# A four-layer transformer on one core: the two parts of x at another address, modulo 256, in the feed-forward sublayers

## The chip, the core and the metric

The kernel runs on one core of a Trainium2 chip. What counts is the time of one execution on the device, in microseconds (us), as a median over runs. The engines are named as in the profile: PE is TensorE's matmul, PEld its load of the stationary operand (the weights of the array), DVE is VectorE, ACT ScalarE, POOL GpSimd, SP SyncE, which issues most of the DMAs.

## The reference

256 tokens of width 1024 go through two blocks of four layers each, in fp32. In the first block a layer is: feed-forward, mixer, feed-forward, each with a norm before and behind. In the second it is a mixer and a feed-forward.

```
for i in range(4):                                   # first block
    x = x + 0.5 * rms_norm(swiglu_ffn(rms_norm(x, g[0]), w_gate_up[i, 0], w_down[i, 0]), g[1])
    x = x + rms_norm(mixer[i](rms_norm(x, g[2]), memory), g[3])
    x = x + 0.5 * rms_norm(swiglu_ffn(rms_norm(x, g[4]), w_gate_up[i, 1], w_down[i, 1]), g[5])
...
for i in range(4):                                   # second block
    x = x + mixer_2[i](rms_norm(x))
    x = x + relu2_mlp(rms_norm(x), w_up[i], w_down[i])
```

The gated feed-forward has 2816 hidden columns, that of the second block 4096. All weights together are some 530 MB and each is used once.

## The kernel before

The residual stream x is kept transposed: 8 row blocks of 128 channels on the partitions, 256 tokens along the row. For precision every operand of a large product is split into two parts of type float32r, hi and lo, and a product is made of three: hi by hi, hi by lo, lo by hi. One product here is one instruction with a stationary operand of 128 by 128 and a moving operand of 128 by (mostly) 256. It is preceded by a weight load for it, which runs beside the product before.

```
def mm3(self, out, xs, ws, first, last):
    nc.tensor.matmul(out, xs[0], ws[0], start=first, stop=False)
    nc.tensor.matmul(out, xs[0], ws[1], start=False, stop=False)
    nc.tensor.matmul(out, xs[1], ws[0], start=False, stop=last)
```

The weights come by DMA into `raw` (3 buffers of 1 MB), ACT makes `whi` of them and DVE `wlo` (4 buffers each, in pieces of 512 columns). The parts of x are the tiles `xThi` and `xTlo`, one of each for the whole kernel. They are written at the end of a sublayer: `handoff` is called as the blocks of the output become ready, and its tasks add to x and write the parts of the next sublayer (`split_x` on ACT, `rest_x` on DVE).

A feed-forward sublayer goes in chunks of 256 hidden columns. `wide` makes the hidden columns: for 2 halves of 128 columns and 8 row blocks, the three products, with the weights stationary and x moving:

```
for j in range(nb):
    b = slice(j * P, (j + 1) * P)
    for k in range(KB):
        self.mm3(ps[:, j * S:(j + 1) * S], (wh[:, k, b], wl[:, k, b]), [z[:, k] for z in self.xTs],
                 k == 0, k == KB - 1)
```

That is 48 products a unit of weights; a gated chunk has two units (gate and up, 96 products), one of the second block has one. The hidden values are split into `hThi`, `hTlo`, and `down` multiplies the chunk before by its rows of the down matrix: 48 products, again with weights stationary and 256 tokens of h moving. The last two chunks go down together (the last down: 24 products of the first of them, then 72 with both). The first part of a sublayer (`early`, 96 products in each) runs while x still arrives. In the mixers x is stationary and the weights move, in widths of 512, 384, 280, 268 or 256 columns; their output goes through `oThi`, `oTlo` as moving operands, as h does in a feed-forward sublayer.

There are 12 feed-forward sublayers. They have 11,520 products with x moving (8 by 11 by 96 and 4 by 16 by 48) and 6528 with h moving at width 256 (the last sublayer takes h as the stationary operand instead). The mixer of the third layer of the second block (a convolution) uses `xThi`, `xTlo` as its own output tiles: 192 more.

Where the tiles lie on a partition is fixed when the program is built. By that table, modulo 256 bytes: `whi`, `wlo`, `xThi`, `xTlo` begin at 96; `hThi`, `hTlo` at 32; the two parts of the memory (`memT`) at 32; `oThi`, `oTlo` at 96 in the second and third mixer of the first block and at 32 in all others. All steps between blocks inside these tiles are multiples of 256 bytes. So the distance of the moving operand from the weights, modulo 256, is 0 for x, 192 for h, and 0 or 192 for o. Where the memory is stationary and weights move, it is 64.

Nearly all instructions are recorded through one helper, so their line in the profile is 160 whatever they do.

Of the kernel before, what the change touches and what calls it, by code (L numbers as in the profile page):

```python
# [9 lines left out]
F32R = mybir.dt.float32r  # L10
# [7 lines left out]
P = 128  # L18
D = 1024
# [29 lines left out]

HALVES = slice(0, 512), slice(512, 1024)  # L50
# [4 lines left out]
def consts():  # L55
    """masks, identity-like matrices and position tables, from the shapes alone"""
# [32 lines left out]
class Clock:  # L89
    """rough times of the engines in us, by which the order of the instructions is chosen"""  # L90
# [10 lines left out]
    def wait(self, until):  # L101
        """the chain of the current stage waits, for data from DRAM or for another chain"""
        if self.chain is not None:
            self.chain = max(self.chain, until)

    def free(self, engine, cost):
        """when the engine has time for an operation"""
        for a, b in self.idle[engine]:
            if max(a, self.now()) + cost <= b:
                return max(a, self.now())  # L110
        return max(self.busy[engine], self.now())

    def reserve(self, engine, start, cost):
        """end of an operation that can start then: it fills a gap between others where one is long enough"""
# [50 lines left out]
class Core:  # L165
    """the engines, with a clock that follows them"""
# [8 lines left out]
class Task:  # L175
    """a chain of stages that is emitted between the large products; a stage ends in a yield: of the engine that has to
    be idle for the next one, of 0 when that waits for other tasks, or of nothing"""
# [5 lines left out]
    def at(self):  # L183
        """when the next stage can begin"""
        return max(self.time, self.clock.busy[self.state] - 0.5) if self.state else self.time
# [12 lines left out]
class Net:  # L198
    def __init__(self, ctx, tc, a):
# [19 lines left out]
        self.xTs = [self.xp.tile([P, KB, S], F32R, name="xT" + n) for n in ("hi", "lo")]  # L219
        self.xT = [[z[:, :, t * P:(t + 1) * P] for z in self.xTs] for t in range(2)]  # L220
# [12 lines left out]

    def begin(self, gain):
        """loads x and the constants and prepares x for the first sublayer"""
# [52 lines left out]
    # ---- tasks  # L288
# [9 lines left out]
    def tick(self):  # L298
        """emits every stage whose inputs should be there by now, then some of the weights to come"""
# [38 lines left out]
    # ---- weights  # L338
    def cols(self, w, ranges, gain=None):
        """all 8 row blocks of the given columns of w, in two units"""  # L340
# [8 lines left out]
    def start(self, units):  # L349
        """units: what is loaded, in the order in which it is taken"""  # L350
# [17 lines left out]
    def load(self):  # L368
        """splits the weights into two exact float32r parts, a piece at a time"""
# [29 lines left out]
    def queue(self, *ins):  # L399
        """issues these behind the last of those that x waits for, on the same engine"""  # L400
        for i, last in zip(ins, self.last):
            self.behind(i, last)

    def behind(self, ins, first):
        """issues ins after first, on the same engine"""
# [4 lines left out]
    def ahead(self, n):  # L410
        """splits the next n units now, before what comes of x with the end of a sublayer"""
# [3 lines left out]
    def take(self, n, more=False):  # L415
        """the next n units; those taken before are through, unless these are more"""
# [8 lines left out]
    def mm3(self, out, xs, ws, first, last):  # L425
        """out (+)= xs.T @ ws for one row block, both as (hi, lo)"""
# [9 lines left out]
    def proj(self, t, units):  # L436
        """tile t's rows of x times the columns in units"""
# [6 lines left out]
    def out_block(self, y, d, blocks, first, last):  # L444
        """block d of y (+)= the transposed output: pairs of weights [128, 1024] and tokens [128, 256], both as (hi, lo).
        Two blocks of a bank are one group: its first product clears the bank for both."""
# [12 lines left out]
    def temp(self):  # L459
        """a row of 1024 for a short time"""  # L460
        return self.nrm.tile([P, KB, S], F32, name="yg", bufs=1).rearrange("p k n -> p (k n)")[:, :D]

    def new_y(self, alone):
        """the blocks of y, and those that share a bank as pairs; the last two have a bank each where they are needed one
        by one"""
# [4 lines left out]
    # ---- transposes  # L470
# [3 lines left out]
    def turn(self, out, src):  # L474
        """out = src transposed: moved, not rounded"""
# [7 lines left out]
    def split_T(self, src, n, pool, tag, hi=None, lo=None, gain=None):  # L483
        """src [128, n*128] in SBUF -> transposed blocks [128, n, 128] as (hi, lo), times the columns gain"""
# [20 lines left out]
    # ---- norms  # L505
    def bcast_row(self, pool, row, name, **kw):
        """a row of DRAM on every partition"""
# [4 lines left out]
    def rsqrt(self, ms, eps, out=None):  # L512
        """(ms + eps) ** -0.5; ms one AP or two to be added"""
# [11 lines left out]
    def square(self, x, scale, out):  # L525
        """out = sum of (scale * x) ** 2 along the row"""
        junk = self.nrm.tile([P, D], BF16, name="junk", bufs=1)
        self.nc.scalar.activation(junk[:, :x.shape[-1]], x, AF.Square, scale=scale, accum_out=out)

    # ---- the residual stream: x transposed, [128, 8 blocks, 256 tokens]  # L530
# [6 lines left out]
    def split_x(self, ks, g):  # L537
        """blocks of x times the gain, their first parts"""
# [5 lines left out]
    def rest_x(self, ks, g):  # L544
        """their second parts, and the squares of pairs"""
# [10 lines left out]
    def leave(self, b):  # L556
        """blocks 2 * b and 2 * b + 1 of the last x, as rows of tokens"""
# [9 lines left out]
    def arriving(self):  # L567
        """(block, part of the weights, part of x) of the products with an x that is still on its way"""
# [13 lines left out]
    def col_sums(self, pc, srcs, first, last):  # L582
        """pc [128, 2] (+)= the sums over the partitions of each [128, 256] of srcs, for each token of both tiles"""
# [6 lines left out]
    def to_rows(self, cols, warm=(0, 0), behind=None):  # L590
        """cols [128, 2], one of a token -> the same on all partitions, [128, 256] in PSUM; before and behind, products
        that nobody reads keep the clock of the tensor engine up while it waits"""
# [15 lines left out]
    def rms(self, deps):  # L608
        """mean square + eps and reciprocal rms of x"""
# [9 lines left out]
    def handoff(self, y, done, end, weight=1.0, rest=None):  # L619
        """x += weight * rms_norm(y) * gain, or x += y, then what the next sublayer needs of x; a product left the next  # L620
        block of y. end: gains of this and of the next norm; rest: mean square + eps of the x by whose rms y still has to
        be divided, or rows by which it still has to be multiplied"""
# [3 lines left out]
        if d == 0:  # L626
            self.out = {"acc": self.nrm.tile([P, 2, S], F32, name="acc", bufs=1), "after": []}
# [39 lines left out]
    def gain_y(self, y, ds, g, o):  # L667
        """blocks ds of y times the gain, and their squares"""
# [66 lines left out]
    # ---- feed-forward  # L735
    FF = 256

    def ffn_steps(self, dff, gated):
        """('part', chunks) and ('down', chunks) in their order; the first part is of two units, the last two chunks go
        down together"""  # L740
# [19 lines left out]
    def ffn(self, w_in, w_down, dff, gated, g_out, g_next):  # L760
# [4 lines left out]
        with tc.tile_pool(name="ff", bufs=3) as fp, tc.tile_pool(name="ff1", bufs=1) as f1:  # L765
# [5 lines left out]
            def scales():  # L771
                """what the reciprocal rms of x still has to be applied with: rows for the gate or for y, the rest of the
                norm of y"""
# [29 lines left out]
            def early():  # L803
                """two units side by side, for x is still on its way"""
# [11 lines left out]
            def wide():  # L816
                """columns of tokens"""
# [78 lines left out]
    # ---- attention pieces  # L896
    def scores(self, ps, q, k, mask=None, extra=()):
        """ps = q.T @ k (+ extra) (+ mask), mask is (column offset, bf16 tile)"""
# [9 lines left out]
    def exp_rows(self, pool, s, scale, den):  # L908
        """exp(scale * (s - max of s)) for each of the b rows of s [128, b, n] in PSUM, den [128, b] gets the sums;
        scale is a number or a column"""  # L910
# [16 lines left out]
    def turn_p(self, pool, p, n, tag="pT"):  # L927
        """the n transposed blocks of p [128, ...]"""
# [10 lines left out]
    def pv(self, out, pT, vs):  # L939
        """out = sum over blocks of p @ v"""  # L940
# [3 lines left out]
    def normalise(self, pool, o, den, heads, t, kb, swapped=False):  # L944
        """o [128, heads * d] in PSUM over den [128, heads], transposed, is from block kb on the input of the output
        projection"""
# [1074 lines left out]
```

## Time and profile before

| | |
|---|---|
| time, median of 3 runs | 3330.47 us (3327.56 to 3331.14) |
| span of the profiled execution, first to last instruction | 3322.9 us |
| PE busy | 3222.2 us, 97% |
| PEld busy | 3073.1 us, 92% |
| DVE busy | 2127.4 us, 64% |
| ACT busy | 1660.6 us, 50% |
| HBM read over the span | 543.82 MB, 165 GB/s |
| mean granted clock of TensorE | 0.990 |

The profiled execution's own time on the device is not listed apart from the three runs; its span is 7.6 us below their median. Matmuls are pipelined, and the ends of their records are modelled: a record of a 256-wide product is some 280 ns long while the next one starts after about 115. So PE's busy share says little. What counts is the distance from one start to the next, here called the pitch: the length of a stretch without pauses over the number of products that start in it. A window of the profile also counts the two products that started before it and are still in flight; they are subtracted.

### The profile page before, as it was taken

How to read it: one execution, taken by the hardware profiler on the slowest of the kernel's cores; microseconds unless marked ns; L12 is line 12 of the kernel's file. 1: busy time of each engine (PE TensorE's matmuls, PEld its weight loads, DVE VectorE, ACT ScalarE, POOL GpSimd, SP SyncE). 2: the span in 40 equal slices, each digit the busy share in tenths (PEclk: the TensorE clock that was granted, in tenths of full speed). 3: DMA queues.
4: the chain of work that ended last, by engine and by line, in shares of the span. 5: the costliest groups of instructions: out<-in, count | busy, mean ns of one | idle time of the engine just before them, and what ended most of it. 6: DMA issues, size and time to landing. Idle time of an engine off the chain costs nothing. (4 is left out here: it accounts for less than half of the span.)

```text
span 3322.9 us, 60453 instructions
## 1 busy us (share of the span) xinstructions
PE 3222.2 (97%) x25108; PEld 3073.1 (92%) x25108; DVE 2127.4 (64%) x3857; ACT 1660.6 (50%) x3375; POOL 261.7 (8%) x237
## 2 busy tenths in 40 slices
PE   8999999999999999999999999999999978999999
PEld 8998999998999997999998998699989967998998
DVE  6557757567757556655657756775666587657754
ACT  6445545445445445544545544554565453545643
POOL 1001000001000000000001001200100051002100
PEclk9999999999999999999999999999999998999999
DMA  7654555544455543454554554535545540554463
GB/s 267 203 183 156 169 184 172 184 127 146 161 183 171 185 153 121 140 190 165 191 190 138 195 184 127 171 123 191 182 147 183 188 142 29 188 191 147 141 197 127
DMA packets 387970, 550.88 MB, mean 166 GB/s; under 512 B 12108, under 2 KB 310956, under 8 KB 387694
## 3 DMA queue, kind: packets, MB, share of 16 engines
q1 hardware_dynamic: 372648, 534.89, 48.9%
q10 hardware_dynamic: 14694, 10.92, 1.1%
q8 instruction: 197, 3.23, 0.4%
q0 software_dynamic: 352, 1.19, 0.2%
q14 instruction: 79, 0.65, 0.1%
HBM read 543.82 MB, written 3.15 MB: 165 GB/s over the span
## 5 line engine op out<-in xcount | busy, mean ns | idle before, releaser
L160 ACT CAST whi<-raw 128x512 fp32r<-128x512 f32 x1996 | 1119.2, 617 | 1108.7 <-issue 945.7
L160 DVE TENSOR_TENSOR wlo<-raw,whi 128x512 fp32r<-128x512 f32 x1996 | 1311.2, 703 | 539.0 <-ACT whi L160 538.2
L160 PE MATMUL ps<-xThi,whi 128*128 128x256 f32 x3904 | 1060.8, 284 | 3.1 <-ACT xThi L160 2.2
L160 PE MATMUL ps<-xTlo,whi 128*128 128x256 f32 x3904 | 1057.7, 283 | 4.0 <-DVE xTlo L160 4.0
L160 PE MATMUL ps<-xThi,wlo 128*128 128x256 f32 x3904 | 1057.6, 283 | 0.0
L160 PEld LDWEIGHTS ps<-xThi,whi 128*128 128x128 f32 x3904 | 727.1, 192 | 7.3 <-ACT xThi L160 6.8
L160 PEld LDWEIGHTS ps<-xTlo,whi 128*128 128x128 f32 x3904 | 727.3, 192 | 5.9 <-DVE xTlo L160 5.4
L160 PEld LDWEIGHTS ps<-xThi,wlo 128*128 128x128 f32 x3904 | 727.4, 192 | 0.0
L160 PE MATMUL ps<-hThi,whi 128*128 128x256 f32 x2176 | 602.4, 277 | 0.0
L160 PE MATMUL ps<-hTlo,whi 128*128 128x256 f32 x2176 | 601.9, 277 | 0.0
L160 PE MATMUL ps<-hThi,wlo 128*128 128x256 f32 x2176 | 601.4, 276 | 0.0
L160 PEld LDWEIGHTS ps<-hTlo,whi 128*128 128x128 f32 x2176 | 409.2, 188 | 0.0
L160 PEld LDWEIGHTS ps<-hThi,whi 128*128 128x128 f32 x2176 | 409.0, 188 | 0.0
L160 PEld LDWEIGHTS ps<-hThi,wlo 128*128 128x128 f32 x2176 | 408.8, 188 | 0.0
L160 PE MATMUL ps<-whi,xThi 128*128 128x512 f32 (+4 forms) x688 | 255.3, 386 | 4.6 <-ACT xThi L160 4.6
L160 PE MATMUL ps<-whi,xTlo 128*128 128x512 f32 (+4 forms) x688 | 245.5, 372 | 5.0 <-DVE xTlo L160 5.0
L160 PE MATMUL ps<-wlo,xThi 128*128 128x512 f32 (+4 forms) x688 | 245.0, 372 | 2.1 <-DVE wlo L160 1.9
L160 DVE TENSOR_TENSOR act<-ps,rows 128x512 f32<-128x512 f32 x88 | 60.8, 690 | 198.9 <-PE ps L160 198.9
L160 DVE TENSOR_TENSOR h<-ps,act 128x512 f32<-128x512 f32 x88 | 60.8, 691 | 174.5 <-PE ps L160 171.3
L160 POOL TENSOR_TENSOR acc<-acc,sq 128x512 f32<-128x512 f32 x60 | 98.1, 1634 | 862.7 <-issue 645.7
L160 PEld LDWEIGHTS ps<-whi,xTlo 128*128 128x128 f32 x688 | 130.3, 191 | 26.7 <-DVE xTlo L160 7.1
L160 PEld LDWEIGHTS ps<-whi,xThi 128*128 128x128 f32 x688 | 130.4, 192 | 26.3 <-ACT xThi L160 8.2
(334 smaller groups left out, 3496.9 us busy)
## 6 DMA issues: line engine op xcount, KB each, us to landing
raw<-in_ffn_w_gate_up_dram SPq DMA_DIRECT2D x176, 1024.0 KB, 5.1
raw<-in_ffn_w_down_dram SPq DMA_DIRECT2D x88, 1024.0 KB, 4.9
raw<-in_mlp_w_up_dram SPq DMA_DIRECT2D x64, 1024.0 KB, 5.5
raw<-in_mlp_w_down_dram SPq DMA_DIRECT2D x64, 1024.0 KB, 4.9
raw<-in_a_w_in_dram SPq DMA_DIRECT2D x12, 1024.0 KB, 5.2
raw<-in_sb_w_in_dram SPq DMA_DIRECT2D x12, 1024.0 KB, 5.2
raw<-in_moba_w_in_dram SPq DMA_DIRECT2D x12, 1024.0 KB, 5.1
raw<-in_b_w_in_dram SPq DMA_DIRECT2D x36, 256.0 KB, 3.5
```

What stands on the lines that cost most here:

```text
L160: return f(*args, **kw)
```

## The change

`xThi` and `xTlo` become tiles with 64 spare elements (256 bytes) behind them, and a view of x is laid into them at an offset that `place` chooses for each sublayer, when its x begins to be written. In feed-forward sublayers it is 28 or 48 elements of 4 bytes, 112 or 192 bytes; in the mixers it is 0, and in the convolution 64 elements, 256 bytes. For `ffn` the first of a layer's two has 28 and the second 48; for `mlp` layers 0 and 2 have 28, layers 1 and 3 have 48. That makes 5760 products with x moving at distance 112 and 5760 at 192. To make room a scratch tile (`junk`) shrinks to 128 columns, and the memory's preparation has one of its own.

```
+SPARE = 64
+X_AT = {"ffn": (28, 48), "mlp": (28, 48), "mix": (0, 0), "mix2": (0, 64)}
...
-        self.xTs = [self.xp.tile([P, KB, S], F32R, name="xT" + n) for n in ("hi", "lo")]
-        self.xT = [[z[:, :, t * P:(t + 1) * P] for z in self.xTs] for t in range(2)]
+        self.room = [self.xp.tile([P, KB * S + SPARE], F32R, name="xT" + n) for n in ("hi", "lo")]
...
+    def place(self, step):
+        at = X_AT[step[0]][step[-1] % 2 if step[0] != "mix2" else step[1] == 2]
+        self.xTs = [z[:, at:at + KB * S].rearrange("p (k n) -> p k n", k=KB) for z in self.room]
+        self.xT = [[z[:, :, t * P:(t + 1) * P] for z in self.xTs] for t in range(2)]
...
     def handoff(self, y, done, end, weight=1.0, rest=None):
...
         if d == 0:
+            if self.following is not None:
+                self.place(self.following)
...
-    def square(self, x, scale, out):
-        junk = self.nrm.tile([P, D], BF16, name="junk", bufs=1)
+    def square(self, x, scale, out, junk=None):
+        if junk is None:
+            junk = self.nrm.tile([P, P], BF16, name="junk", bufs=1)
...
-                self.square(m, 1.0 / 32.0, ms)
+                self.square(m, 1.0 / 32.0, ms, mt.tile([P, D], BF16, name="junk"))
...
     net.start(units)
+    net.place(plan[0])
...
+        net.following = plan[n + 1] if n + 1 < len(plan) else None
```

The rest of the diff takes out comments. In the built programs the instructions of every engine stand in the same order, and on PE, DVE and SP each has the same waits with the same counts; ACT has one wait less and POOL two that name other DMA queues, at the preparation of the memory and of one mixer. Every tile behind `xTlo` in memory moves by a multiple of 256 bytes (1280 for those of the sublayers). So h keeps its distance of 192 and o and the memory keep theirs.

## Rows read from the trace of the kernel before

**Rows 1.** The page, part 1: busy time of PE over the span.

```profile
span 3322.9 us, 60453 instructions
...
PE 3222.2 (97%) x25108; PEld 3073.1 (92%) x25108; DVE 2127.4 (64%) x3857; ACT 1660.6 (50%) x3375; POOL 261.7 (8%) x237
```

**Rows 2.** The page, part 5: groups of products and weight loads.

```profile
## 5 line engine op out<-in xcount | busy, mean ns | idle before, releaser
...
L160 PE MATMUL ps<-xThi,wlo 128*128 128x256 f32 x3904 | 1057.6, 283 | 0.0
...
L160 PEld LDWEIGHTS ps<-xThi,wlo 128*128 128x128 f32 x3904 | 727.4, 192 | 0.0
...
L160 PE MATMUL ps<-hThi,wlo 128*128 128x256 f32 x2176 | 601.4, 276 | 0.0
...
L160 PEld LDWEIGHTS ps<-hThi,wlo 128*128 128x128 f32 x2176 | 408.8, 188 | 0.0
```

**Rows 3.** Windows of the trace: steady chunks of the first feed-forward sublayer.

```profile
core 0: us, PE busy (x) PEld busy (x) DVE busy (x) ACT busy (x) POOL busy (x), PEclk, DMA share, GB/s
91.80:239.00 147.20, 147.20 (x1251) 147.20 (x1249) 80.74 (x129) 65.66 (x121) 0.00 (x0) 1.00 0.57 187
```

**Rows 4.** Windows: one chunk's products with x, then those with h.

```profile
91.80:103.30 11.50, 11.50 (x98) 11.50 (x97) 5.68 (x9) 4.89 (x9) 0.00 (x0) 1.00 0.58 197
103.31:108.75 5.44, 5.44 (x50) 5.44 (x49) 3.70 (x6) 2.71 (x5) 0.00 (x0) 1.00 0.53 163
```

**Rows 5.** Windows: most of the last down of two feed-forward sublayers.

```profile
242.09:250.09 8.00, 8.00 (x70) 8.00 (x69) 4.89 (x11) 2.18 (x4) 0.00 (x0) 1.00 0.43 133
525.13:532.83 7.70, 7.70 (x70) 7.70 (x69) 4.79 (x11) 2.19 (x4) 0.00 (x0) 1.00 0.42 138
```

**Rows 6.** Windows of 6 us in the eleven last downs, three shown.

```profile
243.00:249.00 6.00, 6.00 (x53) 6.00 (x52) 3.10 (x7) 1.79 (x3) 0.00 (x0) 1.00 0.57 178
526.00:532.00 6.00, 6.00 (x55) 6.00 (x55) 3.26 (x7) 2.01 (x4) 0.00 (x0) 1.00 0.54 178
...
3008.80:3014.80 6.00, 6.00 (x56) 6.00 (x55) 5.05 (x9) 2.87 (x6) 0.57 (x1) 1.00 0.55 175
```

**Rows 7.** Windows: output projections of a mixer with o at 192, with o at 0.

```profile
320.01:337.08 17.07, 17.07 (x147) 17.07 (x146) 7.50 (x14) 6.06 (x11) 0.00 (x0) 1.00 0.67 221
1355.85:1374.31 18.46, 18.46 (x156) 18.46 (x155) 7.61 (x14) 6.40 (x12) 0.00 (x0) 1.00 0.44 153
```

**Rows 8.** Windows of PE: two stretches of 256-wide products, memory stationary, distance 64.

```profile
21.60:25.60 4.00, 4.00 (x37) 1.00 1.00 343
35.00:39.00 4.00, 4.00 (x36) 1.00 0.25 95
```

**Rows 9.** Timeline of PE, third mixer, 268-wide, x stationary: every third product.

```profile
1254.21 0.28 PE L160 MATMUL ps<-whi,xThi 128*128 128x268 f32 x1
...
1254.58 0.28 PE L160 MATMUL ps<-whi,xThi 128*128 128x268 f32 x1
...
1254.94 0.28 PE L160 MATMUL ps<-whi,xThi 128*128 128x268 f32 x1
...
1255.31 0.29 PE L160 MATMUL ps<-whi,xThi 128*128 128x268 f32 x1
...
1255.69 0.28 PE L160 MATMUL ps<-whi,xThi 128*128 128x268 f32 x1
```

**Rows 10.** Windows: the first part of the second feed-forward sublayer.

```profile
343.31:360.32 17.01, 15.69 (x126) 15.08 (x126) 16.98 (x29) 11.67 (x23) 6.34 (x5) 1.00 0.14 47
```

**Rows 11.** Timeline and groups of PE: bf16 products that nobody reads.

```profile
253.07 1.69 PE L160 MATMUL ps<-cb 128*128 128x256 bf16 x14
...
L160 PE MATMUL ps<-cb 128*128 128x256 bf16 x300 | 38.7, 273 | 0.0
```

**Rows 12.** The page, part 6: DMA issues, KB each, median us to landing.

```profile
raw<-in_ffn_w_gate_up_dram SPq DMA_DIRECT2D x176, 1024.0 KB, 5.1
```

## The prediction

> **What bounds the kernel now.** I read the page's busy times first: PE is busy for nearly all of the span [rows 1], but its records overlap, so that only says where to look. [...] The groups of the page then show something that the code does not: products of one shape, 128 by 256 with a stationary operand of 128 by 128, have records of 283 ns where x moves and 276 where h moves, and their weight loads 192 against 188, all with no idle time before them [rows 2]. The modelled ends make the lengths useless as times, but their difference is real: in one chunk 96 products with x take 11.50 us, a pitch of 119.8 ns, and the 48 with h right behind them 5.44 us, 113.3 ns [rows 4], the two in flight subtracted. With the hand-over at each end of those 48 I take 113.8 for h.
>
> What differs between x and h there is the tile that moves. By the addresses x lies at distance 0 from the weights, modulo 256, and h at 192. The output projections are the check, since they run the same code in both ways: with o at distance 0 their pitch is 18.46/154 = 119.9 ns, that of x, and with o at 192 it is 17.07/145 = 117.7 [rows 7]. So at distance 0 a product of this shape always costs 120 ns, and at 192 less, but not always equally less. The last downs show the same split, in one tile at one distance: 8.00/68 = 117.6 ns in the first sublayer and 7.70/68 = 113.2 in the second [rows 5]. I call these the slow and the fast phase of distance 192. A phase lasts through tens of products. Of the eleven last downs four run in the slow one (53 or 54 products counted in 6 us) and seven in the fast one (55 or 56) [rows 6]. Distance 64 has both too, with 37 and 36 counted in 4 us [rows 8].
>
> **The change, part by part.** No instruction is added, removed or moved on PE, DVE or SP, and no wait of theirs changes; the one wait less on ACT and the two others on POOL stand outside the feed-forward sublayers. I cost these at nothing. So the whole change is the pitch of 11,520 products, half of them at distance 112 and half at 192. The 96 of each sublayer's first part (1152) wait for x: in the second sublayer's first 17.01 us DVE is busy for 16.98 [rows 10], and a faster product there is hidden behind it. I count half of them: 10,944 products, 5472 at each distance. The ends are none and all of them, 5% either way.
>
> *The half at 192.* The rows for it are direct, h at the same distance in the same shape. Fast phase: 119.8 - 113.8 = 6.0 ns saved, by 5472 = 32.8 us. Slow phase: 119.8 - 117.6 = 2.2 ns, 12.0 us. But there is a price that the diff does not show. Today every down follows products at distance 0, and then h is in the fast phase. With x and h both at 192 the stream has one distance throughout, and a slow phase can run on into h: 2880 products with h lie in these sublayers (four of `ffn` with 528 each, one `mlp` with 768; the last `mlp` has h stationary), 3.8 ns each, 10.9 us. So a half at 192 that is slow throughout gives back nearly all that it gains: 1.1 us. The last downs are the only long streams at 192 that no pause precedes, so I take their share, 7 of 11 fast: 7/11 by 32.8 plus 4/11 by 1.1 = 21.3 us. The bounds are 1 and 33 us.
>
> *The half at 112.* No row has this distance in this shape. The nearest by shape are 64 and 192, on both sides of it, and both have a fast phase of 113 ns [rows 5, 8]. The nearest by distance are products 268 wide, with x stationary, whose distance goes through 0, 48, 96 and 144 in turn: three of each take 0.37, 0.36, 0.37 and 0.38 us [rows 9]. There 96 costs as much as 0 and 144 costs 3.3 ns more a product, so these rows speak against a gain. The bounds are therefore 6.0 ns saved and 3.3 ns lost. I take the saving, since the shape seems to matter more than nearness: the 268-wide products differ by 3 ns or less between neighbouring distances, the 256-wide ones by 6 between 0 and both 64 and 192. No slow phase is counted, because here x (112) and h (192) alternate every 96 and 48 products, as 0 and 192 do now, where h is fast behind every switch. That gives 5472 by 6.0 = 32.8 us; the other end is a loss of 18 us.
>
> *What the faster stream meets.* A chunk of 16.9 us becomes 16.3. DVE's share goes from 55% to 57% and the DMA's rate from 187 GB/s to some 194 [rows 3]; an output projection already runs for 17 us at 221 GB/s [rows 7], and a megabyte lands in 5.1 us [rows 12] where one is wanted every 5.4. So neither becomes the bound. If the DMA's rate stayed at 187, the whole gain would go into waits of PE.
>
> **The sum**: 32.8 + 21.3 = 54.1 us. The profiled span is 3322.9 and becomes 3269; the 7.6 us between it and the median stay. 3330.5 - 54.1 = 3276 us.
>
> **The rivals.**
>
> All fast: the half at 192 keeps the fast phase throughout, as seven of eleven last downs do [rows 6]. 32.8 + 32.8: 3265 us.
>
> One half alone pays: 112 costs as much as 0, as 96 does in the 268-wide products [rows 9], and the other half gives 21: 3309. Or 192 runs slow throughout, as the output projection at 192 does for 17 us [rows 7], and 112 gives 33: 3297.
>
> Faster than h: bf16 products of width 256 have a pitch of (1.69 - 0.27)/13 = 0.109 us [rows 11]. h at its best is 4 ns above it, and if 112 took that away too it would save 10.8 ns by 5472 = 59 us, with 21 for the other half: 3250.
>
> Slower: distance 112 is worse than 0. If the delay has steps of the 6 ns that lie between h and x, and 112 costs one step more, the half loses 33 us; less the 21 of the other half that is 3342. It decides from (21.3 + 6.7)/5472 = 5.1 ns on; the only rows near it show 3.3 at 144 [rows 9], which would give 3327.
>
> No change: the address of a moving operand has no part in it, and x is slower than h for another reason, such as 24 products in a row into one place of PSUM against 6. Against it stands that output projections, with one order of products, run at 120 and at 118 ns [rows 7]. 3330 us.
>
> [...]
>
> **How the numbers follow.** The forecast, 0.33; all fast, 0.25; one half alone, 0.16; faster than h, 0.10: all these are faster by over 0.2% (6.7 us, about what a measurement of this kernel can tell from no change), together 0.84. No change, 0.07, with what cancels to within 6.7 us. Slower, 0.09. The range reaches down below the 3250 of the fastest case by the 5% of the first parts (4 us) and some of the spread of the runs, to 3244, and up past the 3309 of one half alone and its lower bound, a half at 192 that is slow for longer, to 3322. It leaves out no change and slower, 0.16 in all. The forecast's own range is 3265 to 3297, the other cases on its two sides.
>
> **What would show it.** The groups of products with x should drop from 283 ns towards 276 and their weight loads from 192 towards 188. Windows at the same place in a first and in a second feed-forward sublayer of a layer tell 112 from 192: 96 products in 10.9 us if fast, 11.3 if slow, 11.5 if nothing changes. The downs of the second ones tell whether the slow phase runs into h: 48 in 5.46 or 5.64 us. Waits of PE for `whi`, `wlo` or `raw` in these windows would show a new bound. I am wrong if 112 stays at 120 ns or above, if h slows down in all second sublayers, or if mixers change by more than a few us, since nothing of theirs moves modulo 256.

## The result, and the profile after

The changed kernel takes 3277.3 us (median of 4 runs, 3273.0 to 3286.3), the kernel before 3330.8 (4 runs on the same chip, 3327.6 to 3334.7): a ratio of 0.984 (0.983 to 0.986), 53.5 us less. 3276 was forecast. The runs of the changed kernel spread over 13 us, those of before over 7; where the spread comes from is shown below.

The profiled execution took 3273.0 us, its span 3271.2. First its page: the busy times, and of part 5 the groups that answer to [rows 2].

```profile
span 3271.2 us, 60452 instructions
...
PE 3170.2 (97%) x25108; PEld 3021.1 (92%) x25108; DVE 2127.9 (65%) x3857; ACT 1660.7 (51%) x3375; POOL 262.7 (8%) x237
...
L163 PE MATMUL ps<-xThi,wlo 128*128 128x256 f32 x3904 | 1033.6, 277 | 0.0
...
L163 PEld LDWEIGHTS ps<-xThi,wlo 128*128 128x128 f32 x3904 | 713.2, 188 | 0.0
...
L163 PE MATMUL ps<-hThi,wlo 128*128 128x256 f32 x2176 | 601.8, 277 | 0.0
...
L163 PEld LDWEIGHTS ps<-hThi,wlo 128*128 128x128 f32 x2176 | 408.7, 188 | 0.0
```

PE's busy time falls by 52.0 us and the span by 51.7; DVE and ACT have the same busy time as before [rows 1]. The group with x has come down from 283 ns to 277, that with h has not moved, and the weight loads with x now have the 188 ns that h always had. Neither has idle time in front of it. The two other groups with x, which take it as it arrives, had 3.1 and 4.0 us of idle time before and have 4.2 and 4.9 now. So no new wait took the place of the delay.

Next, windows of single chunks in three sublayers: the 96 products with x, then the 48 with h behind them (two in flight are counted with each). The columns are those of [rows 3].

```profile
91.82:102.76 10.94, 10.94 (x98) 10.94 (x97) 5.68 (x9) 4.89 (x9) 0.00 (x0) 1.00 0.59 202
102.77:108.21 5.44, 5.44 (x50) 5.44 (x49) 3.70 (x6) 2.71 (x5) 0.00 (x0) 1.00 0.57 181
369.49:380.79 11.30, 11.30 (x98) 11.30 (x97) 5.69 (x9) 4.89 (x9) 0.00 (x0) 1.00 0.62 199
380.80:386.44 5.64, 5.64 (x50) 5.64 (x49) 3.70 (x6) 2.71 (x5) 0.00 (x0) 1.00 0.57 176
875.15:886.02 10.87, 10.87 (x98) 10.87 (x97) 5.68 (x9) 4.90 (x9) 0.00 (x0) 1.00 0.66 216
886.03:891.46 5.43, 5.43 (x50) 5.43 (x49) 3.70 (x6) 2.71 (x5) 0.00 (x0) 1.00 0.59 187
```

The first pair is the first sublayer, x at 112: 10.94/96 = 114.0 ns where [rows 4] have 119.8. The second pair is the second sublayer, x at 192 in the slow phase: 117.7 ns, and h behind it slow as well, 117.5, where it was 113.3. The third pair is the second sublayer of the second layer, x at 192 in the fast phase: 113.2 and 113.1.

The 114.0 of the first pair is a mean of two things. Split behind the eleventh product (windows of PE: the time from the span's start, its length, PE busy (products), the granted clock, the DMA's share and GB/s):

```profile
91.82:93.13 1.31, 1.31 (x13) 1.00 0.87 309
93.14:102.76 9.62, 9.62 (x87) 1.00 0.55 187
```

The first eleven products behind h take 119 ns each (114 to 130 by their starts), the other 85 take 113.2, as fast as h. So a change from distance 192 to 112 costs some 70 ns once, and then 112 is as good as the fast phase of 192.

Over whole sublayers, from the starts of the products in the trace (first parts left out):

| distance of x | sublayers | pitch of x, ns | pitch of h, ns |
|---|---|---|---|
| 112 | first of each layer, first block | 114.0 to 114.3 | 113.6 to 114.1 |
| 112 | layers 0 and 2, second block | 115.0 to 115.2 | 113.5 |
| 192, slow | second of layer 0 | 117.95 | 117.8 |
| 192, fast | second of layers 1 to 3 | 113.6 | 113.4 |
| 192, fast | layers 1 and 3, second block | 113.8, 114.5 | 113.3 |

Before, x had 119.7 to 120.2 in all twelve. In the second block x at 112 has the higher mean because there 48 products, not 96, share the price of a change of distance.

Measured from the start of one stage to that of the next, the twelve feed-forward sublayers became 59.3 us shorter, and the rest, the mixers above all, 7.6 us longer. The loss in the mixers is one of the granted clock. Windows of PE in the mixer of the second layer, first after, then before, with the columns of the two windows above. Both stretches have the same instructions, 384 columns wide.

```profile
726.00:730.00 4.00, 2.93 (x17) 1.00 0.00 0
730.00:733.00 3.00, 1.21 (x7) 1.00 0.01 3
733.20:736.60 3.40, 3.40 (x13) 0.50 0.18 52
736.70:740.00 3.30, 3.30 (x23) 1.00 1.00 265
```

```profile
737.00:741.00 4.00, 3.01 (x17) 1.00 0.00 0
741.00:744.00 3.00, 1.19 (x7) 1.00 0.01 3
744.00:747.40 3.40, 3.40 (x22) 1.00 0.20 52
747.50:751.00 3.50, 3.50 (x23) 1.00 1.01 275
```

PE did the same in the 7 us ahead, with the same pause, and yet after it the granted clock is at 0.50 for 3.4 us in one execution and at 1.00 in the other: 13 products counted against 22. The mean granted clock of the whole execution is 0.987 against 0.990. Nothing of the change touches these instructions except when they start.

### The profile page after: what moved, and what is told of

Read it like the earlier page. It is cut to its first block, busy times and chain, and to the rows that moved or that the text cites. A ratio compares the mean times of both kernels' runs of the same rounds, so it can differ in the third digit from the quotient of the medians.

```text
span 3271.2 us, 60452 instructions
## 1 busy us (share of the span) xinstructions
PE 3170.2 (97%) x25108; PEld 3021.1 (92%) x25108; DVE 2127.9 (65%) x3857; ACT 1660.7 (51%) x3375; POOL 262.7 (8%) x237
## 5 line engine op out<-in xcount | busy, mean ns | idle before, releaser
L163 PE MATMUL ps<-xThi,whi 128*128 128x256 f32 x3904 | 1038.3, 278 | 4.2 <-ACT xThi L163 4.2
L163 PE MATMUL ps<-xTlo,whi 128*128 128x256 f32 x3904 | 1035.1, 277 | 4.9 <-DVE xTlo L163 4.9
L163 PE MATMUL ps<-xThi,wlo 128*128 128x256 f32 x3904 | 1033.6, 277 | 0.0
L163 PEld LDWEIGHTS ps<-xThi,whi 128*128 128x128 f32 x3904 | 714.2, 188 | 8.0 <-ACT xThi L163 7.4
L163 PEld LDWEIGHTS ps<-xTlo,whi 128*128 128x128 f32 x3904 | 713.0, 188 | 6.8 <-DVE xTlo L163 6.2
L163 PEld LDWEIGHTS ps<-xThi,wlo 128*128 128x128 f32 x3904 | 713.2, 188 | 0.0
```

The source lines that it names most:

```text
L163: return f(*args, **kw)
```

## The experiments

Each edit is against the changed kernel unless another is named; an offset is in elements of 4 bytes. Windows of PE below have the columns of those above, and a pitch is the length over the products counted less two. "By the starts" means the distances between the starts of the single products, which the trace holds to 1 ns.

**All at distance 0.**

```diff
-X_AT = {"ffn": (28, 48), "mlp": (28, 48), "mix": (0, 0), "mix2": (0, 64)}
+X_AT = {"ffn": (0, 0), "mlp": (0, 0), "mix": (0, 0), "mix2": (0, 64)}
```

> The changed kernel with offset 0 in the feed-forward sublayers too: the spare room behind x, the smaller scratch tile and the place of all else stay as changed, only the distance between x and the weights is 0 again. If the distance is the cause: the pitch of products with x is back at 119.8 ns in all 12 sublayers and the time at that of the kernel before, 3331 us within 7. If anything else of the change made the gain (tiles moved, scratch tile, fewer waits): it stays near 3277.

Measured: 3330.1 us (10 runs), a ratio to before of 0.999 (0.9985 to 1.0004). The page's group with x is back:

```profile
L163 PE MATMUL ps<-xThi,wlo 128*128 128x256 f32 x3904 | 1059.1, 283 | 0.0
```

So the spare room, the smaller scratch tile and the changed waits of ACT and POOL are worth nothing, as costed; the offset is all of it.

**One distance everywhere.** In place of (28, 48) for `ffn` and `mlp`, one kernel has (28, 28), 112 bytes, the other (48, 48), 192 bytes.

> Offset 28 elements (112 bytes) in all 12 feed-forward sublayers. If the phase is a matter of one distance for x and h, as I think: no slow phase anywhere, 96 products with x at 114.1 ns and h at 113.5 in every sublayer, and the one sublayer that was slow in the changed kernel's profile (second of the first layer) gains some 5 us: 3270, and the runs lie closer together than the 13 us of the changed kernel. If the slow phase comes by chance at either distance: slow sublayers among the twelve, 3277 with the same spread.

> Offset 48 elements (192 bytes) in all 12. If x and h at one distance make a stream that keeps the phase in which it starts: each sublayer is wholly fast (113.3 ns for x and h) or wholly slow (117.8 for both), slow ones gain nearly nothing, and the time lies between 3265 (none slow) and some 3290 (four slow), with runs that differ by steps of some 6 us. If 192 is simply as good as 112: 3270 with no such steps.

Measured: 3270.3 us at 112 (3269.1 to 3272.9; ratio 0.982, 0.980 to 0.983) and 3285.4 at 192 (3282.4 to 3296.0; 0.987, 0.985 to 0.989). A chunk of the second sublayer with all at 112, which in the changed kernel was the slow one:

```profile
368.84:379.78 10.94, 10.94 (x98) 1.00 0.67 216
379.79:385.22 5.43, 5.43 (x50) 1.00 0.64 193
```

With all at 192, a chunk of the fifth sublayer and one of the fourth:

```profile
1064.03:1075.33 11.30, 11.30 (x98) 1.00 0.61 200
1075.34:1080.98 5.64, 5.64 (x50) 1.00 0.54 167
875.64:886.51 10.87, 10.87 (x98) 1.00 0.68 222
886.52:891.95 5.43, 5.43 (x50) 1.00 0.64 187
```

At 112 all twelve sublayers run alike (x 114.0 to 115.2 ns). At 192 five of twelve are slow throughout, x and h at 117.8 to 118.0; a gated one then takes 189.8 us in place of 183.4. So a slow sublayer costs 6.4 us, and the 13 us of spread among the changed kernel's runs are the size of two of them; that their number can differ from run to run is shown by the second profile below. The execution with these five took 3296.0 us, the longest of the four. 112 is the better half of the change although its mean pitch beside h at 192 is the worse one.

**Other distances, one a sublayer.**

```diff
+FF_AT = {"ffn": (0, 4, 8, 16, 20, 24, 32, 36), "mlp": (40, 44, 56, 64)}
...
+        if step[0] in FF_AT:
+            at = FF_AT[step[0]][2 * step[1] + step[2] if step[0] == "ffn" else step[1]]
```

> Each feed-forward sublayer at a distance of its own: first block 0, 16, 32, 64, 80, 96, 128, 144 bytes, second block 160, 176, 224, 256. If the distance counts modulo 256: 256 is as slow as 0 (119.8 ns), and the pitch falls from there over a few tens of bytes on both sides to 113 or 114. If only an exact coincidence counted: 16 is as fast as 112 already. If the modulus is larger than 256: the sublayer at 256 is fast. If two places 128 apart met as well: 128 is slow too.

Then the neighbours of 112 and 192, with room of 128 elements, so that the last sublayer has 368 bytes, which is 112 modulo 256:

```diff
-SPARE = 64
+SPARE = 128
+FF_AT = {"ffn": (26, 27, 29, 30, 46, 47, 49, 50), "mlp": (12, 52, 60, 92)}
```

> Each sublayer at a distance of its own again: first block 104, 108, 116, 120, 184, 188, 196, 200 bytes, second block 48, 208, 240 and 368, which is 112 modulo 256. If the good distances are single narrow places, as 96 and 128 (120 and 118.8 ns) beside 112 say: 104 and 120 are slow already, or halfway. If 113 to 114 holds over some tens of bytes: all within 8 bytes are fast. If 256 is the modulus at a good place too: the last sublayer runs at 114 to 115; if not, at 117 to 120.

Measured: 3326.2 and 3336.1 us (one run each; the kernel before, on the same two chips, 3331.5 and 3330.3). Chunks of 96 products in the first of the two kernels, at 64, 96 and 128:

```profile
884.26:895.56 11.30, 11.30 (x98) 1.00 0.65 206
1414.04:1425.53 11.49, 11.49 (x98) 1.00 0.61 202
1608.28:1619.66 11.38, 11.38 (x98) 1.00 0.57 199
```

In the second one, at 108, 116, 188 and 196, four bytes on either side of the two places of the change:

```profile
375.07:386.56 11.49, 11.49 (x98) 1.00 0.62 202
569.41:581.11 11.70, 11.70 (x98) 1.00 0.57 193
...
1421.67:1433.05 11.38, 11.38 (x98) 1.00 0.64 200
1615.25:1626.92 11.67, 11.67 (x98) 1.00 0.58 197
```

Mean pitch of x by distance, ns, each from one sublayer of one execution:

| 0 | 16 | 32 | 48 | 64 | 80 | 96 | 104 | 108 | **112** | 116 | 120 |
|---|---|---|---|---|---|---|---|---|---|---|---|
| 119.8 | 118.5 | 116.9 | 118.6 | 118.0 | 118.7 | 120.0 | 120.0 | 120.0 | **114.9** | 122.0 | 122.0 |

| 128 | 144 | 160 | 176 | 184 | 188 | **192** | 196 | 200 | 208 | 224 | 240 |
|---|---|---|---|---|---|---|---|---|---|---|---|
| 118.8 | 116.9 | 117.6 | 119.4 | 120.2 | 118.7 | **113.6 or 117.9** | 121.9 | 120.2 | 119.5 | 118.3 | 117.3 |

(112 is the last sublayer at 368 bytes; with all at 112 bytes it has the same 114.9. 192 is the changed kernel.) 112 and 192 are single places: 4 bytes aside the product costs 5 to 8 ns more than the best there, at 108, 116 and 196 as much as at 0 or more. 256 bytes are as slow as 0: 120.2 ns in a sublayer that had 120.2 at 0 too. So in these two runs the distance counts modulo 256, at a bad place and, with 114.9 ns at 368 bytes as at 112, at a good one. The pitch does fall beside 0, to 116.9 at 32, but of the distances tried only 112 and 192 reach 115 or less. A distance with a slow and a fast phase shows only one of them here; at 64, for instance, [rows 8] have 4.00/35 = 114.3 ns in another stage, with the weights moving.

The downs of these two kernels show one thing more. The 48 products with h behind the chunk at 64 above:

```profile
895.57:901.21 5.64, 5.64 (x50) 1.00 0.54 169
```

That is 117.5 ns: h, at 192 as always, is slow in every down of this sublayer, and so it is behind x at 16, 48, 128, 144 and 200. Each of these is one sublayer of one execution, but behind x at 0 and 112 every down between two chunks was fast, in every profiled execution of this study (113.1 to 113.5 ns in the windows taken). So a change of distance alone does not make h fast; what runs ahead of it counts too.

**The same distances at other addresses.** A pad of 32 bytes ahead of everything else moves weights, x, h and o alike, and x is at 0 in the first sublayers and at 112 in the second ones.

```diff
-X_AT = {"ffn": (28, 48), "mlp": (28, 48), "mix": (0, 0), "mix2": (0, 64)}
+X_AT = {"ffn": (0, 28), "mlp": (0, 28), "mix": (0, 0), "mix2": (0, 64)}
...
+        pad = self.const.tile([P, 8], F32, name="pad")
+        nc.gpsimd.memset(pad, 0.0)
```

> All operands of the products, stationary and moving, lie 32 bytes further in memory than in the changed kernel, modulo 256 (the weights at 128 in place of 96), and x lies at distance 0 from the weights in the first feed-forward sublayers of a layer (and mlp 0 and 2) and at 112 in the second ones (and mlp 1 and 3). If only the distance counts: x at 119.8 to 120.2 ns in the first ones and 114 to 115 in the second ones, h 113.4 to 114.3 everywhere, and a time of 3330 - 5472/2 x 5.7 = some 3300 us. Rival, the moving operand's own address modulo 256 counts (112 was good because x began at 96 + 112 = 208): here the x at distance 112 begins at 240 and the x at 0 begins at 128, so neither is at 208, and x in the second ones should leave 114 to 115 for the 117 to 122 that other places showed, with no gain over 3330.

Measured: 3300.0 us (before 3327.4). A chunk with x at 0, and one with x at 112:

```profile
92.66:104.15 11.49, 11.49 (x98) 1.00 0.59 201
...
391.37:402.31 10.94, 10.94 (x98) 1.00 0.56 196
```

119.7 and 114.0 ns, as without the pad (119.8 and 114.0). So what counts is the distance between the two operands, not where either lies modulo 256; one shift of both was tried.

**The other moving operand.** With all x at 112, h is moved too: by 64 bytes, to distance 0, in one kernel, and by 176 bytes, to 112, in the other. A third adds o at 112.

```diff
-                hT[c] = [fp.tile([P, nb, S], F32R, name="hT" + x, bufs=4) for x in ("hi", "lo")]
+                room = [fp.tile([P, nb * S + SPARE], F32R, name="hT" + x, bufs=4) for x in ("hi", "lo")]
+                hT[c] = [z[:, 16:16 + nb * S].rearrange("p (j n) -> p j n", j=nb) for z in room]
```

> All 12 sublayers with x at 112, and h moved by 64 bytes so that it lies at distance 0 from the weights, where x was. If the distance makes the pitch, whatever the operand: h goes from 113.6 to 120 ns, 6528 products by 6.2 = 40 us slower than 3270, so 3311. If x was slow for something of its own (its order of products, its tile): h stays at 113.6 and the time at 3270.

> All 12 sublayers with x at 112, and h moved so that it lies at 112 too. If the 114.1 to 115.2 ns of x at 112 (against 113.4 to 113.8 in fast sublayers at 192) are the price of changing the distance twice a chunk: both at 113.4, some 11 us less than 3270: 3259, provided no slow phase exists at 112. If a stream with one distance always risks the slow phase, as at 192: slow sublayers, 3275 to 3290. If the 0.7 to 1.4 ns belong to 112 itself: h gets them too, 3275.

> The kernel with x and h at 112, and the inputs of the output projections (o) at 112 as well, 1248 products that now run at 120 or 118 ns. If 112 is good for any moving operand of this width: 3 to 5 us less than with x and h alone. If o is paced by its chain of waits: the same time.

Measured: 3308.6 us with h at 0 (3301.1 to 3311.6), 3262.4 with h at 112 (3261.9 to 3265.5; ratio 0.980, 0.978 to 0.981) and 3259.1 with o there too (3256.2 to 3259.8; 0.978, 0.977 to 0.980). A chunk with h at 0, then one with h at 112:

```profile
91.09:102.02 10.93, 10.93 (x98) 1.00 0.57 196
102.03:107.78 5.75, 5.75 (x50) 1.00 0.56 177
```

```profile
91.18:102.05 10.87, 10.87 (x98) 1.00 0.58 198
102.06:107.49 5.43, 5.43 (x50) 1.00 0.61 188
```

At distance 0 h costs 119.8 ns, as x did: against all x at 112 the kernel loses 38.3 us, where 6528 by 6.4 would be 41.8. The order of the products with h is the same in both, so that is not what makes a moving operand slow. With both at 112 x drops from 114.0 to 113.2 in this chunk, and in all sublayers but the last to 113.3 to 113.7, and no sublayer is slow. So the 114.0 to 115.2 of x at 112 beside h at 192 is the price of changing the distance, and by the starts the first products behind h are as fast as the others here. The gain is 7.9 us where some 11 were expected. Some 2 of the rest are the last sublayer's: there h is stationary, its move takes the distance from 64 to 144, and the 384 products with 512 columns of weights moving go from 229 to 235 ns. o at 112 gives 3.3 us more. The kernel with x, h and o at 112 beats the kernel before by 71 us and the changed one (on another chip) by 18 us.

**Wide products of the mixers**, where x is stationary and the weights move. To the kernel with x, h and o at 112:

```diff
+MIX_AT = {"mix": (36, 0, 48, 16), "mix2": (28, 48, 64, 36)}
...
+        if step[0] in MIX_AT:
+            at = MIX_AT[step[0]][step[1]]
```

> The version with x, h and o at 112, with one more change: the x of the mixers, where x is stationary and the weights move, lies at other offsets, so that the distance of the moving weights from the stationary x is 112, 0, 64, 192 in the four mixers of the first block and 144, 64, 0, 112 in those of the second. If the delay belongs to any pair of a moving and a stationary operand, the wide products change with it: those 512 wide, which take 226 to 227 ns at distance 0, and those of 384, 280 and 268. At 112 and 192 they should then be faster by up to 6 ns a product (some 8 us over 1440 products 512 wide if all were at 112), and at 64 and 144 nearly as at 0. Rival: wide products are not slowed by it, since the delay comes once per weight load and a longer stream covers it; then the pitch of 226 to 227 ns stays at all distances and the time is that of x, h and o at 112, 3259 us, within 6 us.

Measured: 3258.6 us (one run). Stretches of 512-wide products in two mixers of the second block, both at 0 in the kernel with x, h and o at 112:

```profile
2333.96:2347.58 13.62, 13.62 (x62) 1.00 0.37 128
2953.81:2968.11 14.30, 14.30 (x65) 1.00 0.25 61
```

In this kernel the first is at 64 and the last at 112; the one between them, another mixer's, is at 0:

```profile
2332.15:2345.87 13.72, 13.72 (x62) 1.00 0.39 131
2617.96:2631.57 13.61, 13.61 (x62) 1.00 0.39 122
2952.16:2966.85 14.69, 14.69 (x65) 1.00 0.26 70
```

227 ns at 0 in both kernels, 228.7 at 64, 233.2 at 112. The time is that of the rival, but both theories fall: wide products do depend on the distance, so the length of the stream does not cover the delay; but what is good for them is 0, and 112 costs 6 ns more. Stages at 144 and 192 have 233 as well, by the starts of their products. One stage of 57 at 112 ran at 227, so a phase exists there too.

The mixers also have short stretches 256 columns wide, with x stationary and the weights moving. In this kernel, at 112 in the first mixer and at 192 in the fourth:

```profile
304.80:306.84 2.04, 2.04 (x19) 1.00 0.93 373
1780.21:1782.13 1.92, 1.92 (x19) 1.00 1.00 412
```

120 and 113 ns; at 0 they take 120. So with x stationary 112 gives nothing in this one stretch, in the very shape in which it gives 6 ns when x moves. The distance modulo 256 is not all that counts: which operand moves does too, or 112 has a slow phase there.

I estimate all that the 512-wide products lose at some 5 us (some 700 products by 6.2 ns and 480 by 1.6), which this one time does not show; it is within what the clock in the mixers moves.

**Is the slow phase fixed by the program?** The kernel with all x at 192 again, unchanged.

> The kernel with all x at 192 once more, as it was, for a second profile of it. If a sublayer's phase is drawn afresh in every execution, other sublayers should be slow (117.8 to 118 ns for x and h) than the five of the first profile (ffn00, ffn20, ffn21, ffn30, mlp2), and the time lies between 3270 (none slow) and 3345 (all slow). If the program fixes it, the same five are slow and the time is near 3285.

Measured: 3305.6 us, with seven slow sublayers, where the first execution had five and took 3296.0; three of them are slow in both executions. The fourth, fast before, is now slow:

```profile
889.06:900.36 11.30, 11.30 (x98) 1.00 0.63 203
900.37:906.01 5.64, 5.64 (x50) 1.00 0.54 171
```

So the phase is not fixed by the program alone; it can come out differently in each execution, and is kept for a whole sublayer. Six of the twelve changed it. The first sublayer and the four of the second block are among those that did not; whether that is chance two executions can't tell.

**Does a disturbance change it?** To all x at 192, one product of 64 columns in front of each unit's 48, overwritten by the first of them:

```diff
+                nc.tensor.matmul(ps[:, :64], wh[:, 0, :P], self.xTs[0][:, 0, :64], start=True, stop=True)
                 for j in range(nb):
```

> All x at 192, and in front of the 48 products with x of every unit of weights (some 230 units behind the first parts) one more product of 64 columns, which the first of the 48 overwrites: nothing of the result changes, some 230 x 0.04 to 0.11 = 9 to 25 us of work is added. It breaks the even stream of 256-wide products. If the phase is a relation between the streams that lasts until something disturbs it, then within one sublayer units in the slow phase (48 in 5.65 us) and in the fast one (5.44 us) should now follow each other, or all go to one phase. If the phase belongs to the place of the tiles in this execution, whole sublayers stay slow or fast as in the kernel without the extra product, five of twelve slow.

Measured: 3332.5 us, with 216 such products. The 0.04 us for one of them was my estimate, and no run shows it: in the trace of before most products of 64 columns have 110 ns to the next start, and none less than 55. Four downs in a row of the first sublayer, two such products between one and the next:

```profile
86.59:92.23 5.64, 5.64 (x50) 1.00 0.83 266
103.58:109.00 5.42, 5.42 (x50) 1.00 0.57 172
120.54:126.18 5.64, 5.64 (x50) 1.00 0.51 161
137.53:143.17 5.64, 5.64 (x50) 1.00 0.60 168
```

Slow, fast, slow, slow, and on in this order. Unit by unit, one extra product apart, the 48 with x are fast (115.5 ns) in every third unit and slow (119.5) in the two others, through all sublayers but the last, the first unit of each left out. Both are some 2 ns above the values without the extra product, and by the starts that is the first product's doing: the second one starts some 200 ns behind it, where 113 to 118 are usual, and a few products later the units run at 113.3 and 117.8 again. So in this run, at distance 192, one fast and two slow phases follow each other, and one product more moves the stream on by one.

## Why the prediction was right, and where it was not

**What bounds the kernel.** Right: the whole change was costed as pitch, and PE is busy for all of each chunk's window above. The larger shares of DVE (5.68 of 10.94 us with x, before 5.68 of 11.50) and of the DMA (0.57 to 0.66 in the windows above) brought no wait.

**The change without the offset** was costed at nothing; with all at 0 it is 0.999 of before.

**The half at 112.** 32.8 us were summed, from 6.0 ns. Measured 5.7 ns in `ffn` and 4.8 in `mlp`: 28.3 us over the 5184 products outside the first parts, where 6.0 ns would be 31.1. The term was a little too large, by the price of changing the distance: I had taken it over from h, where the hand-over adds 0.5 ns to each of 48 products, 24 ns, and at 112 it is some 70 ns; with h at 112 too it is gone. But the reason I gave is false. I took the saving because 64 and 192 lie on both sides of 112 and are fast. The sweep shows no good region between them: 96 and 108 cost 120 ns, 116 costs 122. The nearest rows by distance, the 268-wide products with nothing gained at 96 [rows 9], were a better guide to the neighbourhood than mine; that 112 itself is good no row showed. (Their weights have steps of 1072 bytes between blocks, 48 modulo 256, so the statement that all steps are multiples of 256 does not hold for them.) The bound for a loss, 3.3 ns at 144, rested on three products and on one step of the 0.01 us in which the rows are given. The next stretch of the same stage, before the change, has 0.36 us for the three at 144:

```profile
1258.75 0.28 PE L160 MATMUL ps<-whi,xThi 128*128 128x268 f32 x1
...
1259.11 0.28 PE L160 MATMUL ps<-whi,xThi 128*128 128x268 f32 x1
```

By the starts it is 382 ns in one stretch and 366 in the other, so these rows show no loss that belongs to 144. Leaving out a slow phase was right by luck too: the reason given, that h is fast behind every switch, does not hold behind x at 16, 48, 64, 128, 144 or 200. The value came out right by a place that I could not have known.

**The half at 192.** 7/11 fast gave 21.3 us. In the profiled execution five of six sublayers were fast: 26.0 us outside the first parts. The mechanism, a slow phase that lasts for a sublayer and runs on into h and then gives back nearly everything, is as forecast: the slow one gains 960 by 2.0 ns and loses 528 by 4.0 ns, so nothing is left. The share is what was uncertain: five of six in this profile, seven and five of twelve with all at 192, 17 of 30 together, near the 19 that 7/11 would give. That is partly luck, since nothing ties the phase of a last down, from which 7/11 came, to that of a sublayer. The last run shows one fast phase in three, and an even draw among them would give 10 of 30; what decides the phase stays open.

**First parts.** Half of their gain was counted. The two halves make 54.3 us, the sublayers gained 59.3. The other 5.0 are the first parts and what h gained in the other sublayers, some 2 us by the starts, most of it in last downs that were slow before and are fast now. That leaves 3 of the 6.8 which 1152 by 5.9 ns would be, so half was about right.

**The sum.** 59.3 us against 54.1, and then 7.6 given back outside, where I had expected no more than a few us. That step failed: I costed what does not move at nothing, but the granted clock in the mixers is not the same from one execution to the next. With the 0.990 and 0.987 of the two executions I estimate the time lost to the lower clock at 33 us before and 43 after (both rounded, so 9 us give or take 3), as much as is missing. The change need not be the cause: over all executions of this study the clock is between 0.987 and 0.991, and one program alone, with x at 112 and h at 0, had all of that range in four executions. In its profiled one, at 0.991, everything outside the feed-forward sublayers took some 2 us less than before. So two profiles can differ by as much as is missing without any change in the mixers; why the clock differs stays open. The two misses nearly cancel, so 3276 is closer than its parts, which is luck; the gap between span and median, taken as 7.6 us, is 6.1 now. Most of that gap is no fixed cost: the profiled execution of the changed kernel took 3273.0 us, 1.8 more than its span, and the other 4.3 are what it was faster than the median.

**The rivals.** "No change", by a reason other than the address, falls with the kernel at 0 (3330.1 us) and with h at 0, which slows to 119.8 ns in its own order of products. "All fast" is missed by the one slow sublayer of the profile, and "one half alone" falls, since both halves paid: 28.3 and 26.0 us. "Faster than h" falls too: no chunk shown here went below 113.1 ns, where h at its best had 113.2 before [rows 5]. "Slower" has something in it, only not at 112 and not by a step of 6 ns: at 116 and 196 the product costs 122 ns, 2 more than at 0. Why the distance between two operands changes the pitch at all no run here shows.

## What to carry to other kernels

When products of one shape have two pitches with no wait in front of them, compare the addresses of the moving and the stationary operand: here 6 ns of 120 hung on their distance modulo 256, and 112 was worth 71 us for x, h and o together. Measure the distance for each shape, don't interpolate it: 4 bytes beside a good place can be worse than where one began (122.0 ns at 116, 119.8 at 0), and 112 was good here for 256 moving columns with the weights stationary (113.2 ns with h there too), but gave nothing where 256 columns of weights moved (120 ns), and cost 6 ns where 512 of them moved. And prefer a place whose pitch is the same in every sublayer (112) to one whose best is as good but which can fall into a slower phase (192, 113.6 or 117.9 ns).

## What was not expected of the hardware

The good places are narrow (108: 120.0 ns; 112: 114 to 115; 116: 122.0), hold at another address of both operands, and differ with the shape and with the operand that moves: 512 columns of weights take 227 ns at 0 and 233 at 112.

What ran just before counts. Behind a change from 192 to 112 eleven products take 119 ns and the rest 113, and h at 192 takes 113 ns behind x at 0 or 112, but took 118 behind x at 64 and at five other distances.

At 192 the 48 products of a unit take 115.5, 119.5 and 119.5 ns each in turn where an extra product of 64 columns stands ahead of each unit: it moves the stream on by one phase. The large products come in threes (hi by hi, hi by lo, lo by hi), which may be why there are three; no run changed that number.

After equal pauses with equal work ahead the granted clock fell to 0.50 in one execution and stayed at 1.00 in another.
